# Layer one of a two-layer decoder: the gate computed as [channel, token] and applied after the outputs' transposition, the state updates issued directly behind their products

## The chip, the cores and the metric

The kernel runs on one core of one Trainium2 chip. The metric is the device time of one execution in microseconds (us); the number before is the median of three runs.

Five engines work side by side: PE (TensorE, the matrix engine; PEld is its weight load), DVE (VectorE), ACT (ScalarE), POOL (GpSimd) and SP (SyncE, which here issues all the DMAs). Each works through its own queue in order and waits for others by semaphores.

## The reference, cut to what matters

One sequence of 1024 tokens, model width 1024, mixer width 2048 in 16 heads of 128. Layer one (HGRN2) projects the normalised input into q, forget logits f, values i (v below) and a gate g, runs a gated recurrence over chunks of 64 tokens, normalises each head's output over its 128 channels, and multiplies it by silu(g) before the output projection:

```
q, fz, i, g = jnp.split(h @ w_in, 4, axis=-1)
...
o = _rms(o, onorm_g.reshape(A_HEADS, HEAD_DIM)).reshape(bsz, s, WIDTH).astype(h.dtype)
return (o * jax.nn.silu(g)) @ w_out
```

Layer two (FoX) is a forgetting attention over shared keys and values. The change touches layer one alone.

## The kernel before, in words

All products use float32r operands split into an exact high and low half, so each product of two matrices is three matmuls (high by high, high by low, low by high). `hT(th, k, lo)` is the transposed normalised input, in halves of 512 tokens (`th`) and k-tiles of 128.

There are two forms of a projection. `gemm_T` keeps 128 columns of the weight stationary and moves 512 tokens, so its result is [128 channels, 512 tokens]; one call is 24 matmuls of 128x512. `gemm_N` keeps 128 tokens stationary and moves 256 weight columns, so its result is [128 tokens, 256 channels]; one call covers two token tiles and is 48 matmuls of 128x256. Four calls of either do one projection of a pair of heads over all 1024 tokens.

Layer one goes over eight pairs of heads (`hg_pair`, p = 0 to 7). The main stream of a pair is v (`gemm_N`), g (`gemm_N`), then for each half of the tokens f and q of the pair's two heads (`gemm_T`). `put_g` makes silu(g): a sigmoid on ACT (L577) and a product on DVE (L578). For pair 0, v and half of g grow with the pieces of `hT` while the modulation columns are still being made (`grow`, `lay`).

Beside it run threads. `hg_half(p, th)` does for one half of the tokens: `hg_att` (scores within pairs of chunks and the keys turned round), `hg_state` (the products of keys and values, in PSUM bank `pu`), `hg_out` (the outputs, in bank `po`, normalised by `rsqrt_mean`), and `hg_turn` (the outputs transposed to [channel, token] and stored to `ogd`). The half th = 0 of a pair runs beside the pair's own f and q of th = 1, the half th = 1 beside the next pair's v and g.

The class `Weave` sets PE's order: the main stream calls `tick` with the us that it has laid down, and a thread's next step is put in as soon as its due time is past. PE's order is strict. The order on DVE, ACT, POOL and SP is set when the program is built, by a scheduler that places each instruction by when it estimates that it can run; `tc.high_priority()` raises some.

Names and lines for the steps below. In `hg_forget`: Ln on ACT (L457), the running sum on DVE (L458, a scan), small copies into `dl` (L464 to L466), differences (L467, L468) which the exponentials on ACT (L472) wait for. In `hg_out`: the first state (L520, a copy out of `pu`) and the later ones (L522), each read by the next output matmul; the sums of squares (L525, L527), `rsqrt_mean` (L213 to L219), the scaling (L529, DVE) and the gate's product (L531, POOL, two pieces of 128x256 for each head). In `hg_turn`: the transposes (on PE, recorded at L51), their copy out (L539, ACT) and four stores (L541, SP). `mod_sum` (L260, L263, DVE) works on modulation weights of later layers that stream in beside. `split_w` makes a weight's halves: high on ACT (L224), low on POOL (L225), 128x1024 in each of two pieces; the raw tile is then free for the next load (L236, SP).

Of the kernel before, what the change touches and what calls it, by code (L numbers as in the profile page):

```python
# [8 lines left out]
F32 = mybir.dt.float32  # L9
# [21 lines left out]
class Weave:  # L31
    """The order of the tensor engine: the products of one stream, with the steps of others put in
    between them once enough of the stream has gone by to cover what they wait for."""
# [28 lines left out]
    def tick(self, us):  # L62
        """us of the main stream have been laid down"""
        self.now += us
        while True:
            due = [th for th in self.threads if th[0] <= self.now]
            if not due:
                return
            self._step(min(due, key=lambda th: th[0]))

    def need(self, mark):
        """run the steps on until this mark has been set"""
        while mark not in self.marks:
            assert self.threads, mark
            self._step(self.threads[0])
# [7 lines left out]
def hybrid_trunk_kernel(ctx: ExitStack, tc: tile.TileContext, x, c, mod_w, mod_b, norm_g, a_w_in,  # L83
# [82 lines left out]
    keep = cst.tile([P, P], I32, name="keep")        # 1 where column >= partition  # L166
    V.memset(keep, 1)
    G.affine_select(keep, keep, [[1, P]], ALU.is_ge, 0, base=0, channel_multiplier=-1)
    rows4k = cst.tile([P, D], F32, name="rows4k")    # chunk-reset mask, gate rows, rows of -F
# [38 lines left out]
    def rsqrt_mean(ss, n, inv):  # L208
        """1/sqrt(ss*inv + EPS) on [P, n]: a guess from the exponent, three Newton steps"""
# [12 lines left out]
    def halves(eng, hi, lo, src):  # L222
        """src as a sum of two float32r parts, exactly"""
# [3 lines left out]
    # raw tiles of streamed weights: a list of sources in the order of their use, two loads ahead  # L227
# [12 lines left out]
    def raw_next():  # L240
        """the block of the next raw tile"""
# [7 lines left out]
    def mod_src(b):  # L249
        """modulation weights of output blocks b, b+1 of 128: layer 0, layer 1, kv"""  # L250
# [6 lines left out]
    def mod_sum(*todo):  # L257
        """acc = sum over k-tiles of silu(c) * w, still over partitions, for each (raw tile, acc)"""
# [6 lines left out]
    def mod_cols(b, acc, ps):  # L265
        """mcol[:, b:b+2] = silu(c) @ w + bias"""
# [5 lines left out]
    # h^T as exact float32r halves: block th*4 + k//2, [hi | lo], each [P, 2, 512]  # L272
# [3 lines left out]
    def gscale(gc, sc, k0, k1, g):  # L276
        """g[:, k0:k1] = norm gain * (1 + scale)"""
# [4 lines left out]
    def split_w(eng=None, more=True):  # L282
        """the next raw weight, 256 columns, as exact halves -> accessors of their k-tiles"""
# [9 lines left out]

    def gemm_T(ps, w, j, th):
        """ps[128 outputs, 512 tokens] from columns j*128.. of w"""
        js = slice(j * P, (j + 1) * P)
        for k in range(KT):
            wh, wl = w[0](k)[:, js], w[1](k)[:, js]
            PE.matmul(ps, lhsT=wh, rhs=hT(th, k, 0), start=(k == 0), stop=False)
            PE.matmul(ps, lhsT=wh, rhs=hT(th, k, 1), start=False, stop=False)  # L300
            PE.matmul(ps, lhsT=wl, rhs=hT(th, k, 0), start=False, stop=(k == KT - 1))
            PE.tick(0.65)
# [8 lines left out]
    def gemm_N(ps, w, t):  # L311
        """ps[128 tokens, all columns of w] of token tiles t and t+1"""
# [41 lines left out]
    def h_piece(k, th):  # L354
        """h^T of k-tile k for half of the tokens"""
# [6 lines left out]

    # first weights: v of pair 0 for all tokens and g for half of them grow with the k-tiles of h^T;
    # two token tiles grow side by side in a bank, so a product with zeros opens all of it
# [6 lines left out]
    for ps in vps + gps:  # L371
        PE.matmul(ps, lhsT=zeros[:, 0:P], rhs=zeros, start=True, stop=False)

    def grow(banks, w, i, ts):
        return [(banks, w, k, t) for k in (2 * i, 2 * i + 1) for t in ts]

    def lay(products, pieces):
        """pieces of h^T, with products between them"""
        n = -(-len(products) // len(pieces)) if pieces else len(products)
        while products or pieces:  # L380
            if pieces:
                h_piece(*pieces.pop(0))
            for banks, w, k, t in products[:n]:
                gemm_Nk(c256(banks[t // 2])[:, t % 2, :], w, t, k, False)
# [5 lines left out]
    for i in range(4):  # L390
# [10 lines left out]
        if i == 0:  # L401
            wv = split_w(G, more=False)
            lay([], [(k, 0) for k in ks])
            lay(grow(vps, wv, 0, range(4)), [])
            lay([], [(k, 1) for k in ks])
            ready = grow(vps, wv, 0, range(4, NT))
            continue
        if i == 1:
            wg = split_w(G, more=False)
            ready += grow(gps, wg, 0, range(4))  # L410
        lay(ready, [(k, th) for k in ks for th in range(2)])
        ready = grow(vps, wv, i, range(NT)) + grow(gps, wg, i, range(4))
    lay(ready, [])

    # the other small vectors
# [4 lines left out]
    # lower bound of the first layer: first row of a softmax over the two rows of logits  # L420
# [13 lines left out]
    # units of 512 columns in blocks 18..24  # L434
# [755 lines left out]
```

## Time and profile before

| | us |
|---|---|
| median of three runs (2415.35, 2417.05, 2423.49) | 2417.05 |
| span of the profiled execution | 2421.3 |
| PE busy in it | 2321.1 (96%) |
| DVE busy | 1367.2 (56%) |
| ACT busy | 1004.3 (41%) |
| POOL busy | 594.3 (25%) |

The profile is of one execution. Its span, from the first to the last instruction, is 4.25 us over the median and inside the range of the three runs; what lies around the span is not recorded apart. Layer one's pairs run from about 110 to 1020 us of the span, and a pair takes about 118 us. L48 and L51 are the lines of a helper through which every matmul and every transpose goes, so on PE the tile tells which product it is: `mm` are projections, `oa` outputs, `sm` scores, states and transposes.

### The profile page before, as it was taken

The numbers are of one execution on the slowest core, as the hardware profiler recorded it, in microseconds if no ns is written. First come the engines' busy times: TensorE is split into PE (matmuls) and PEld (weight loads), VectorE is DVE, ScalarE is ACT, GpSimd is POOL, SyncE is SP. The second block draws the span as 40 slices with busy tenths as digits, with TensorE's granted clock in tenths as the row PEclk, the third lists the DMA queues.
The fourth block names the chain that finished last, engine by engine and source line by source line (L and its number), as shares of the span: only waits on it lengthen the run. The fifth ranks groups of instructions, "written<-read, shape, count | busy, mean of one in ns | idle before, by whom it ended". The sixth has DMA issues, their size and how long they took to land.

```text
span 2421.3 us, 39983 instructions
## 1 busy us (share of the span) xinstructions
PE 2321.1 (96%) x15530; PEld 2109.8 (87%) x15530; DVE 1367.2 (56%) x3587; ACT 1004.3 (41%) x1646; POOL 594.3 (25%) x543
## 2 busy tenths in 40 slices
PE   4999999999999999999999999999999999999999
PEld 3889888888888888788899999989999999998887
DVE  7565655555655555746752113267667766777533
ACT  5453444444344435333422222334554544455321
POOL 3222222222222121101321212243343433333000
PEclk9999999999999999999999999999999999999999
DMA  8213131313131313565523322332222322235443
GB/s 276 90 43 98 44 96 45 96 44 97 45 96 53 95 53 108 168 212 173 173 75 111 92 70 83 118 90 85 73 85 63 96 74 85 63 95 176 154 139 116
DMA packets 219970, 245.04 MB, mean 101 GB/s; under 512 B 14547, under 2 KB 182645, under 8 KB 219781
## 3 DMA queue, kind: packets, MB, share of 16 engines
q1 hardware_dynamic: 219780, 242.49, 32.3%
q8 instruction: 122, 2.00, 0.3%
q14 instruction: 68, 0.55, 0.1%
HBM read 196.22 MB, written 46.21 MB: 100 GB/s over the span
## 4 chain that ended last, share of the span: by engine, by line
PE 74%; DVE 12%; ACT 5%; DMA 3%; issue 3%; POOL 2%; SPq 0%; DVEq 0%; ACTq 0%; POOLq 0%
PE mm L48 57%; PE sm L48 6%; PE oa L48 6%; PE sm L51 5%; POOL blk L225 1%; DVE dl L464 1%; DVE rs_y L219 1%; DMA blk<-in_mod_w_dram 1%; DVE blk L225 1%; DVE blk L263 1%; ACT L457 1%; DVE blk L458 1%; DVE rows4k L263 1%; DVE rs_t L214 1%; DVE rs_t L218 1%
## 5 line engine op out<-in xcount | busy, mean ns | idle before, releaser
L48 PE MATMUL mm<-blk,blk 128*128 128x256 f32 (+1 forms) x11408 | 1932.1, 325 | 9.7 <-DVE blk L225 5.3
L48 PEld LDWEIGHTS mm<-blk,blk 128*128 128x128 f32 x11408 | 1650.0, 192 | 158.1 <-DVE blk L225 8.5
L225 POOL TENSOR_TENSOR blk<-blk,blk 128x1024 fp32r<-128x1024 f32 (+1 forms) x134 | 313.9, 2353 | 678.3 <-ACT blk L224 524.3
L224 ACT ACTIVATE blk<-blk 128x1024 fp32r<-128x1024 f32 (+3 forms) x352 | 305.3, 881 | 406.1 <-PE mm L48 264.2
L225 DVE TENSOR_TENSOR blk<-blk,blk 128x1024 fp32r<-128x1024 f32 (+3 forms) x218 | 206.4, 954 | 194.0 <-ACT blk L224 183.1
L51 PE MATMUL sm<-ident,blk 128*128 128x128 f32 x1201 | 188.1, 276 | 36.2 <-POOL blk L531 11.8
L48 PE MATMUL oa<-blk,blk 128*128 128x256 f32 (+1 forms) x1248 | 187.5, 286 | 26.3 <-DVE blk L520 14.6
L48 PE MATMUL sm<-blk,blk 128*128 128x128 f32 (+5 forms) x1456 | 208.6, 301 | 1.3 <-ACT blk L492 1.2
L48 PEld LDWEIGHTS oa<-blk,blk 128*128 128x128 f32 x1248 | 169.9, 193 | 38.2 <-DVE blk L520 15.9
L51 PEld LDWEIGHTS sm<-ident,blk 128*128 128x128 f32 x1201 | 142.0, 141 | 64.5 <-issue 20.6
L48 PEld LDWEIGHTS sm<-blk,blk 128*128 128x128 f32 (+1 forms) x1456 | 168.1, 172 | 19.6 <-issue 3.5
L1034 ACT ACTIVATE blk<-blk,m 128x128 f32<-128x128 f32 (+7 forms) x128 | 99.0, 774 | 127.2 <-DVE m L1032 119.2
L879 DVE TENSOR_REDUCE sst<-blk 128x4 f32<-128x512 f32 x32 | 21.8, 682 | 215.4 <-ACT blk L878 215.4
L1036 POOL TENSOR_SCALAR blk<-blk,smx 128x128 f32<-128x128 f32 (+7 forms) x128 | 98.1, 766 | 136.4 <-DVE smx L1035 123.3
L225 DVE TENSOR_TENSOR blk<-sm,blk 128x512 fp32r<-128x512 f32 (+1 forms) x160 | 92.9, 581 | 62.3 <-ACT blk L224 61.9
L263 DVE SCALAR_TENSOR_TENSOR blk<-blk,cc,blk 128x256 f32<-128x256 f32 x196 | 106.9, 548 | 26.0 <-DMA blk<-in_mod_w_dram 17.2
L1006 POOL TENSOR_TENSOR blk<-rows4k,keep 128x128 f32<-128x128 f32 x128 | 61.5, 480 | 238.0 <-DVE mx L1013 207.7
L224 ACT ACTIVATE blk<-sm 128x512 fp32r<-128x512 f32 (+1 forms) x160 | 81.1, 507 | 48.5 <-PE sm L51 47.8
L1013 DVE CUSTOM_DVE_ANT_0 blk<-sm,rows4k 128x128 f32<-128x128 f32 (+3 forms) x176 | 84.6, 494 | 22.9 <-PE sm L48 21.3
L459 POOL TENSOR_SCALAR blk<-blk,cc 128x512 f32<-128x512 f32 x32 | 23.8, 744 | 251.7 <-ACT blk L456 251.7
L531 POOL TENSOR_TENSOR blk<-blk,blk 128x256 f32<-128x256 f32 x64 | 47.6, 764 | 151.1 <-DVE blk L529 131.4
L472 ACT ACT_TABLE_LOAD x31 | 39.8, 1283 | 102.7 <-DVE blk L467 102.7
(156 smaller groups left out, 1657.4 us busy)
## 6 DMA issues: line engine op xcount, KB each, us to landing
blk<-in_a_w_in_dram SPq DMA_DIRECT2D x64, 512.0 KB, 3.8
blk<-in_mod_w_dram SPq DMA_DIRECT2D x48, 512.0 KB, 4.8
blk<-in_kv_w_dram SPq DMA_DIRECT2D x32, 512.0 KB, 4.5
blk<-in_b_w_in_dram SPq DMA_DIRECT2D x32, 512.0 KB, 3.9
ogd<-blk SPq DMA_DIRECT2D x128, 64.0 KB, 2.2
blk<-in_kv_mod_w_dram SPq DMA_DIRECT2D x16, 512.0 KB, 3.4
blk<-in_a_w_out_dram SPq DMA_DIRECT2D x16, 512.0 KB, 4.9
blk<-ogd SPq DMA_DIRECT2D x16, 512.0 KB, 4.7
```

The lines of the kernel that those rows point to most:

```text
L48: self._chain(self.PE.matmul(*a, **k))
L51: self._chain(self.PE.transpose(*a, **k))
L214: V.tensor_scalar(t.bitcast(I32), m.bitcast(I32), 1, None, ALU.logical_shift_right)
L224: S.activation(hi, src, AF.Copy)
L225: eng.tensor_tensor(lo, src, hi.bitcast(F32), ALU.subtract)
L263: V.scalar_tensor_tensor(acc, rawk(rb, k), csil[:, k:k + 1], acc, ALU.mult, ALU.add)
L472: S.activation(lf[:, :, 1, :], lf[:, :, 1, :], AF.Exp)
L531: G.tensor_tensor(c128(sq)[:, 2 * q:2 * q + 2, :], c128(sq)[:, 2 * q:2 * q + 2, :], sg(th * 4 + 2 * q)[:, :, js], ALU.mult)
L1006: G.tensor_tensor(nfm, nF[:, i * P:n], negm, ALU.add)
L1013: V.tensor_tensor_reduce(dst, src, add, 1.0, -3e38, ALU.add, ALU.max, mx[:, nm:nm + 1])
L1034: S.activation(l[:, 0:n], l[:, 0:n], AF.Exp, bias=m, accum_out=sm)
L1036: G.tensor_scalar(l[:, 0:n], l[:, 0:n], sm, 0.0, ALU.mult, ALU.add)
```

## The change

`gemm_T`'s inner step becomes a function `gemm_Tk`. The gate g is computed by `gemm_T` instead of `gemm_N`, for pair 0's grown half too, and lies as [channel, token] in its block. Its product leaves `hg_out` and is done in `hg_turn`, on the transposed outputs (L545, POOL, one piece of 128x512 for each head), in front of the stores. The state updates move from `hg_out` to `hg_state`, behind the products and under `high_priority`, and `hg_half` first runs the steps on until the previous half's last outputs are laid down. Comments are dropped (not shown).

```
+    def gemm_Tk(ps, w, j, th, k):
+        js = slice(j * P, (j + 1) * P)
+        wh, wl = w[0](k)[:, js], w[1](k)[:, js]
+        PE.matmul(ps, lhsT=wh, rhs=hT(th, k, 0), start=(k == 0), stop=False)
+        PE.matmul(ps, lhsT=wh, rhs=hT(th, k, 1), start=False, stop=False)
+        PE.matmul(ps, lhsT=wl, rhs=hT(th, k, 0), start=False, stop=(k == KT - 1))
...
-    for ps in vps + gps:
+    for ps in vps:
...
+    def grow_g(i):
+        return [(lambda k=k, j=j: gemm_Tk(gps[j], wg, j, 0, k)) for k in (2 * i, 2 * i + 1) for j in range(2)]
...
     def hg_state(j, th, v):
...
-        u["pu"] = pu
-
-    def hg_out(h, j, th, v, sg):
+        with tc.high_priority():
+            if th == 1:
+                V.tensor_scalar(st[:, 0, :], st[:, 0, :], dl[:, 0:1], None, ALU.mult)
+            for n in range(nl):
+                if th == 0 and n == 0:
+                    V.tensor_copy(st[:, 1, :], pu[:, 0:P])
+                else:
+                    V.scalar_tensor_tensor(st[:, (n + 1) % 4, :], st[:, n, :], dl[:, 4 + n:5 + n],
+                                           pu[:, n * P:(n + 1) * P], ALU.mult, ALU.add)
+
+    def hg_out(h, j, th, v):
...
-        for q in range(2):
-            G.tensor_tensor(c128(sq)[:, 2 * q:2 * q + 2, :], c128(sq)[:, 2 * q:2 * q + 2, :],
-                            sg(th * 4 + 2 * q)[:, :, js], ALU.mult)
-
-    def hg_turn(h, j, th):
+
+    def hg_turn(h, j, th, sg):
...
         S.activation(u["ogT"], pg, AF.Copy, scale=ongc[:, h:h + 1])
+        G.tensor_tensor(u["ogT"], u["ogT"], sg(j, th), ALU.mult)
...
+        if p > 0 or th == 1:
+            PE.need(("out", p - 1 + th, 1, 1 - th))
         for j in range(2):
             hg_state(j, th, v)
...
-        for t in range(4 if p == 0 else 0, NT, 2):
-            ps = mm_ps()
-            gemm_N(ps, wg, t)
-            put_g(ps, t)
+        for th in range(1 if p == 0 else 0, 2):
+            for j in range(2):
+                ps = mm_ps()
+                gemm_T(ps, wg, j, th)
+                put_g(ps, j, th)
```

On PE, this is where the gate's products begin beside the half (p = 3, th = 1), just ahead of its second head's outputs. Before (the moving operand stands first behind the arrow: weight blocks 89 to 92, stationary tokens in 71 to 74):

```order
L48 MATMUL mm<-blk_0_89,blk_0_71 128x256
L48 MATMUL mm<-blk_0_91,blk_0_71 128x256
L48 MATMUL mm<-blk_0_89,blk_1_72 128x256
L48 MATMUL mm<-blk_1_90,blk_0_73 128x256
L48 MATMUL mm<-blk_1_92,blk_0_73 128x256
L48 MATMUL mm<-blk_1_90,blk_1_74 128x256
```

Of the change (tokens 69 to 72 move, the weight 89 and 91 is stationary):

```order
L48 MATMUL mm<-blk_0_69,blk_0_89 128x512
L48 MATMUL mm<-blk_1_70,blk_0_89 128x512
L48 MATMUL mm<-blk_0_69,blk_0_91 128x512
L48 MATMUL mm<-blk_0_71,blk_0_89 128x512
L48 MATMUL mm<-blk_1_72,blk_0_89 128x512
L48 MATMUL mm<-blk_0_71,blk_0_91 128x512
```

Half as many matmuls, each twice as wide, stand in the gate's place; where the other products stand between them stays as it was but for a few products' shift.

On DVE, this is the end of the second head's forget work of pair 3, th = 1, where the states of the half (3, 0) are updated (blk_0_115 and blk_1_116 hold the states of the two heads, sm is `pu`). Before:

```order
L458 SCALAR_TENSOR_TENSOR blk_0_107<-rows4k,blk_0_105 128x512
L520 COPY blk_0_115<-sm 128x128
L464 COPY dl<-blk_0_107 128x4
L465 COPY dl<-blk_0_107 128x1
L466 TENSOR_TENSOR dl<-blk_0_107 128x3
L522 SCALAR_TENSOR_TENSOR blk_0_115<-blk_0_115,dl,sm 128x128
L467 TENSOR_TENSOR blk_0_105<-dl,blk_0_107 128x4x64
L468 TENSOR_TENSOR blk_0_107<-blk_0_107,dl 128x4x64
L522 SCALAR_TENSOR_TENSOR blk_0_115<-blk_0_115,dl,sm 128x128
```

Of the change (L465 is the scan, L515 and L517 the states, L471 to L475 the work on `dl` and the differences):

```order
L465 SCALAR_TENSOR_TENSOR blk_0_107<-rows4k,blk_0_105 128x512
L515 COPY blk_0_115<-sm 128x128
L471 COPY dl<-blk_0_107 128x4
L472 COPY dl<-blk_0_107 128x1
L517 SCALAR_TENSOR_TENSOR blk_0_115<-blk_0_115,dl,sm 128x128
L515 COPY blk_1_116<-sm 128x128
L517 SCALAR_TENSOR_TENSOR blk_0_115<-blk_0_115,dl,sm 128x128
L473 TENSOR_TENSOR dl<-blk_0_107 128x3
L517 SCALAR_TENSOR_TENSOR blk_0_115<-blk_0_115,dl,sm 128x128
L474 TENSOR_TENSOR blk_0_105<-dl,blk_0_107 128x4x64
```

The first update stands behind the scan in both; the later ones have moved up past L466 and ahead of the difference (now L474).

On POOL, these are the gate's products of pair 3 among the low halves of weights. Before (L531 is the gate, L225 the low half of a weight piece):

```order
L531 TENSOR_TENSOR blk_1_112<-blk_1_112,blk_0_103 128x256 x2
L225 TENSOR_TENSOR blk_1_92<-blk_1_96,blk_1_90 128x1024
L531 TENSOR_TENSOR blk_1_112<-blk_1_112,blk_0_103 128x256 x2
L225 TENSOR_TENSOR blk_0_87<-blk_0_93,blk_0_85 128x1024
L531 TENSOR_TENSOR blk_1_112<-blk_1_112,blk_1_104 128x256 x2
L225 TENSOR_TENSOR blk_1_88<-blk_1_94,blk_1_86 128x1024
L531 TENSOR_TENSOR blk_1_112<-blk_1_112,blk_1_104 128x256 x2
```

Of the change (L545 is the gate):

```order
L225 TENSOR_TENSOR blk_1_92<-blk_1_96,blk_1_90 128x1024
L545 TENSOR_TENSOR blk_0_117<-blk_0_117,blk_0_103 128x512
L545 TENSOR_TENSOR blk_0_117<-blk_0_117,blk_1_104 128x512
L225 TENSOR_TENSOR blk_0_87<-blk_0_93,blk_0_85 128x1024
L225 TENSOR_TENSOR blk_1_88<-blk_1_94,blk_1_86 128x1024
L545 TENSOR_TENSOR blk_0_117<-blk_0_117,blk_0_103 128x512
L545 TENSOR_TENSOR blk_0_117<-blk_0_117,blk_1_104 128x512
```

The second low half of each weight now stands directly behind the first, ahead of the gate's products. One more exchange, on DVE: `put_g`'s first product of the next pair (before L578, now L585) stood behind the scaling L529 of the second head's th = 1 outputs and now stands ahead of it (now L536).

## Rows read from the trace of the kernel before

**Rows 1.** The page: busy us (share of the span) and instructions.
```profile
PE 2321.1 (96%) x15530; PEld 2109.8 (87%) x15530; DVE 1367.2 (56%) x3587; ACT 1004.3 (41%) x1646; POOL 594.3 (25%) x543
```
**Rows 2.** Groups by form: busy us, mean ns, idle before, what ended it.
```profile
L51 PE MATMUL sm<-ident,blk 128*128 128x128 f32 x1201 | 188.1, 276 | 36.2 <-POOL blk L531 11.8 <-DMA blk<-in_x_dram 9.8 <-DVE blk L883 6.1
...
L48 PE MATMUL oa<-blk,blk 128*128 128x128 f32 x480 | 68.1, 290 | 25.8 <-DVE blk L520 14.6 <-DVE blk L522 11.2
```
**Rows 3.** Timeline of PE, a pair: start, us, instruction, [idle before <-releaser].
```profile
501.39 0.71 PE L48 MATMUL oa<-blk,blk 128*128 128x128 f32 x4 [2.08 <-DVE blk L520]
503.64 1.73 PE L48 MATMUL oa<-blk,blk 128*128 128x128 f32 x6 [1.54 <-DVE blk L522]
...
555.17 3.84 PE L48 MATMUL mm<-blk,blk 128*128 128x256 f32 x30
560.74 0.44 PE L51 MATMUL sm<-ident,blk 128*128 128x128 f32 x2 [1.74 <-POOL blk L531]
561.47 0.46 PE L51 MATMUL sm<-ident,blk 128*128 128x128 f32 x2 [0.30 <-POOL blk L531]
```
**Rows 4.** Chain that ended last, stretches of 256 and of 512 columns: start, us.
```profile
520.64 4.31 PE mm L48 x36
...
594.72 5.49 PE mm L48 x24
```
**Rows 5.** Timeline of DVE: around the wait at 501 us, and later.
```profile
499.79 1.22 DVE L458 TENSOR_TENSOR_SCAN blk<-rows4k,blk 128x512 f32<-128x512 f32 x1 [3.26 <-ACT blk L457]
501.05 0.29 DVE L520 COPY blk<-sm 128x128 f32<-128x128 f32 x1
501.25 1.95 DVE L464 COPY dl<-blk 128x4 f32<-128x4 f32 x1
...
503.18 0.15 DVE L466 TENSOR_TENSOR dl<-blk 128x3 f32<-128x3 f32 x1
...
559.73 0.68 DVE L578 TENSOR_TENSOR blk<-mm,blk 128x512 f32<-128x512 f32 x1
...
584.42 0.17 DVE L464 COPY dl<-blk 128x4 f32<-128x4 f32 x1
```
**Rows 6.** The chain between 546 and 561 us.
```profile
548.65 2.38 POOL blk L225
551.04 4.59 DMA blk<-in_mod_w_dram
...
555.72 0.49 DVE blk L263
...
559.12 0.70 DVE blk L529
...
560.64 0.79 POOL blk L531
```
**Rows 7.** Timeline of POOL.
```profile
500.84 2.34 POOL L225 TENSOR_TENSOR blk<-blk,blk 128x1024 fp32r<-128x1024 f32 x1 [2.42 <-ACT blk L224]
...
543.26 2.40 POOL L225 TENSOR_TENSOR blk<-blk,blk 128x1024 fp32r<-128x1024 f32 x1 [20.02 <-issue]
```
**Rows 8.** Clock windows of PE: stretch, us, PE busy (x), PEclk, DMA share, GB/s.
```profile
210.20:213.60 3.40, 3.40 (x18) 0.50 0.48 128
797.30:800.70 3.40, 3.40 (x19) 0.50 0.37 104
565.20:568.60 3.40, 3.40 (x30) 1.00 0.96 281
...
619.80:626.60 6.80, 5.66 (x18) 0.50 0.25 80
```
**Rows 9.** DVE and POOL at the end of the pairs.
```profile
986.79 2.32 POOL L531 TENSOR_TENSOR blk<-blk,blk 128x256 f32<-128x256 f32 x2 [19.75 <-DVE rs_y L215]
...
987.74 0.70 DVE L217 SCALAR_TENSOR_TENSOR rs_t<-rs_y 128x4 f32<-128x4 f32 x1
```
**Rows 10.** SP's queue: DMA issues.
```profile
563.23 2.06 SPq L541 DMA_DIRECT2D ogd<-blk  x4
565.38 0.43 SPq L236 DMA_DIRECT2D blk<-in_a_w_in_dram  x1
```

More of the change, by code (lines that the diff above doesn't have):

```diff
@@ L292, in split_w @@
         return (lambda k: ar(8 + 2 * i, k * 256, 256, F32R)), (lambda k: ar(9 + 2 * i, k * 256, 256, F32R))
+    def gemm_Tk(ps, w, j, th, k):
[4 more added lines that the diff above has]
+        PE.matmul(ps, lhsT=wl, rhs=hT(th, k, 0), start=False, stop=(k == KT - 1))
     def gemm_T(ps, w, j, th):
-        js = slice(j * P, (j + 1) * P)
         for k in range(KT):
[L298 to L301, printed above, removed]
+            gemm_Tk(ps, w, j, th, k)
             PE.tick(0.65)
@@ L370, in hybrid_trunk_kernel, with grow_v @@
     gps = [sm_ps(), sm_ps()]
-    for ps in vps + gps:
+    for ps in vps:
         PE.matmul(ps, lhsT=zeros[:, 0:P], rhs=zeros, start=True, stop=False)
-    def grow(banks, w, i, ts):
-        return [(banks, w, k, t) for k in (2 * i, 2 * i + 1) for t in ts]
+    def grow_v(i, ts):
+        return [(lambda k=k, t=t: gemm_Nk(c256(vps[t // 2])[:, t % 2, :], wv, t, k, False))
+                for k in (2 * i, 2 * i + 1) for t in ts]
+    def grow_g(i):
+        return [(lambda k=k, j=j: gemm_Tk(gps[j], wg, j, 0, k)) for k in (2 * i, 2 * i + 1) for j in range(2)]
     def lay(products, pieces):
@@ L382, in lay @@
                 h_piece(*pieces.pop(0))
-            for banks, w, k, t in products[:n]:
-                gemm_Nk(c256(banks[t // 2])[:, t % 2, :], w, t, k, False)
+            for product in products[:n]:
+                product()
             del products[:n]
@@ L403, in hybrid_trunk_kernel @@
             lay([], [(k, 0) for k in ks])
-            lay(grow(vps, wv, 0, range(4)), [])
+            lay(grow_v(0, range(4)), [])
             lay([], [(k, 1) for k in ks])
-            ready = grow(vps, wv, 0, range(4, NT))
+            ready = grow_v(0, range(4, NT))
             continue
@@ L409, in hybrid_trunk_kernel @@
             wg = split_w(G, more=False)
-            ready += grow(gps, wg, 0, range(4))
+            ready += grow_g(0)
         lay(ready, [(k, th) for k in ks for th in range(2)])
-        ready = grow(vps, wv, i, range(NT)) + grow(gps, wg, i, range(4))
+        ready = grow_v(i, range(NT)) + grow_g(i)
     lay(ready, [])
@@ L507, in hg_out @@
         pov = c128(po)
-        att, qd, st, dl, pu = u["att"], c128(u["qd"]), c128(u["S"]), u["dl"], u["pu"]
+        att, qd, st = u["att"], c128(u["qd"]), c128(u["S"])
         js = slice(j * P, (j + 1) * P)
-        if th == 1:
-            V.tensor_scalar(st[:, 0, :], st[:, 0, :], dl[:, 0:1], None, ALU.mult)
         for n in range(4):
@@ L516, in hg_out @@
                 PE.matmul(pov[:, n, :], lhsT=qd[:, n, :], rhs=st[:, n, :], start=False, stop=True)
-            if n == 3 and th == 1:
-                break
-            if first:
-                V.tensor_copy(st[:, 1, :], pu[:, 0:P])
-            else:
-                V.scalar_tensor_tensor(st[:, (n + 1) % 4, :], st[:, n, :], dl[:, 4 + n:5 + n],
-                                       pu[:, n * P:(n + 1) * P], ALU.mult, ALU.add)
         sq = u["sq"]
@@ L553, in hg_half @@
         for j in range(2):
-            hg_out(2 * p + j, j, th, v, sg)
+            hg_out(2 * p + j, j, th, v)
             PE.marks.add(("out", p, j, th))
@@ L558, in hg_half @@
         for j in range(2):
-            hg_turn(2 * p + j, j, th)
+            hg_turn(2 * p + j, j, th, sg)
             yield 3.0
@@ L567, in v, with sg, put_g @@
             return ar(bv, t * 256, 256)
-        def sg(t):
-            return c256(ar(bg, t * 256, 512))
+        def sg(j, th):
+            return ar(bg, j * 1024 + th * 512, 512)
         def put_v(ps, t):
             S.activation(ar(bv, t * 256, 512), ps, AF.Copy)
-        def put_g(ps, t):
-            s = ar(bg, t * 256, 512)
-            S.activation(s, ps, AF.Sigmoid)
-            V.tensor_tensor(s, ps, s, ALU.mult)
+        def put_g(ps, j, th):
+            S.activation(sg(j, th), ps, AF.Sigmoid)
+            V.tensor_tensor(sg(j, th), ps, sg(j, th), ALU.mult)
         if p == 0:
@@ L582, in hg_pair @@
                 put_v(vps[t // 2], t)
-            for t in range(0, 4, 2):
-                put_g(gps[t // 2], t)
+            for j in range(2):
+                put_g(gps[j], j, 0)
         else:
@@ L590, in hg_pair @@
         wf = split_w()
-        for t in range(4 if p == 0 else 0, NT, 2):
-            ps = mm_ps()
-            gemm_N(ps, wg, t)
-            put_g(ps, t)
+        for th in range(1 if p == 0 else 0, 2):
+            for j in range(2):
+                ps = mm_ps()
+                gemm_T(ps, wg, j, th)
+                put_g(ps, j, th)
         wq = split_w()
```

## The prediction

> **What bounds the kernel now.** I read the page first: PE is busy for 2321.1 of 2421.3 us [rows 1], so time comes off in three ways only: PE's products take less of it, PE waits less, or its clock is higher. Then the groups of PE by form, for what it waits for in layer one [rows 2]. Two groups matter. The output products (`oa`) wait 25.8 us, for the first states of L520 and the later ones of L522. The transposes (`sm` from `ident`) wait 11.8 us for POOL's gate product of L531; the rest of that group's waits are elsewhere. The timeline of one pair shows where these lie [rows 3]: 2.08 and 1.54 us in front of output products at 501 us, and 1.74 and 0.30 us in front of the second head's transposes at 560 us. Third the clock [rows 8]: 565.2 to 568.6 us holds 30 matmuls of 256 columns at a granted clock of 1.00, the same 3.4 us behind a transposes' wait 18 or 19 at 0.50. [...]
>
> **(a) The gate's products.** A pair's g was 4 calls of 48 matmuls of 128x256, and is 4 calls of 24 of 128x512: 96 a pair, 768 in all. The columns streamed are the same; what can change is the price per instruction. The chain has 36 matmuls of 256 in 4.31 us, 119.7 ns each, and 24 of 512 in 5.49 us, 228.8 ns each [rows 4]. A 512 replaces two 256s and saves 2 x 119.7 - 228.8 = 10.6 ns; x 768 = **8.1 us**. Bounds: a stretch's end is modelled, and taking the 36 as 120 ns or a little less moves the saving by some 20%; pair 0's grown half (48 of the 768) partly stands beside waits, where nothing is won. I keep 6 to 10 us.
>
> [...]
>
> **(b) The transposes' wait.** The second head's transposes are wanted at 559.01 (555.17 + 3.84) and start at 560.74 [rows 3]. They wait for the last link of this chain [rows 6]: the second low half of a weight on POOL (548.65, 2.38 us), which frees the raw block for a load of modulation weights (551.04, 4.59 us), which `mod_sum` on DVE needs at 555.72; behind that in DVE's queue come the Newton steps and the scaling L529 (559.12, 0.70), then L531 (560.64, 0.79). The second pieces of L531 give the 0.30.
>
> After the change the transposes read the scaling's output directly: the 0.79 us of L531 and the 0.30 drop out of PE's path. And on POOL the second low half stands right behind the first, no longer behind the first head's gate. The first runs from 543.26 for 2.40 us [rows 7], so the second can run from 545.66 instead of 548.65: 2.99 us earlier, and with it the load, `mod_sum` and the scaling. Against this, `put_g`'s product, 0.68 us [rows 5], now stands ahead of the scaling. The scaling then ends near 559.82 - 2.99 + 0.68 = 557.5. PE wants it at 559.0 less what (a) has saved in this pair, at most 96 x 10.6 ns = 1.0 us: 558.0. That leaves 0.5 us to spare. What may eat it: while POOL multiplies, small DVE operations can be held up: during L531 at 986.79, L217 took 0.70 us [rows 9], against 0.15 for L466, as small, elsewhere [rows 5]. The first head's new product L545 (I estimate 1.5 us, two pieces of 0.79) runs just among the second head's Newton steps. So a little of the wait can remain: of 11.8 us in seven pairs I leave 0.25 each, and take **10.0 us**. Bounds: 11.8 if nothing holds DVE up, 0 if all of it comes back (rival C).
>
> [...]
>
> **(c) The clock behind those waits.** Three of the seven pairs' waits are followed by 3.4 us at 0.50; the first and the last of the three are shown [rows 8]. Such a stretch does 18 or 19 matmuls instead of 30, so it loses some 11.3 x 0.12 = 1.36 us; three give **4.1 us**. I take it whole, as the wait goes nearly whole; lower bound 0, if the remainder of the wait is enough to lower the clock.
>
> **(d) The state updates.** At 501 us DVE's scan L458 starts at 499.79, having waited 3.26 us for ACT's logarithm, and the state copy L520 stands behind it at 501.05 [rows 5]; PE's output product starts at 501.39 [rows 3]. In the new order the copy (L515) still stands directly behind the scan (now L465), as the excerpt shows: the 2.08 us stay. The second wait, 1.54 us, is for L522, which stood behind L464, and L464 took 1.95 us because POOL's low half ran from 500.84 for 2.34 us [rows 5, 7]. In the new order that small copy (now L471) still stands between the first and the second update; only L466 (0.15 us) has moved behind it. Its start-to-start share can be at most 0.15, at least 0; I take half, in seven pairs (14.6 / 2.08, [rows 2, 3]): **0.5 us**. The clock's falls behind these waits stay as well.
>
> **Costs that I take as nothing.** Three updates now stand ahead of the difference L474, which the exponentials on ACT need; they cost at most three copies' 0.29 us [rows 5], 0.9 us. The first products that read those exponentials come behind pair p + 1's v, and 520 us is still all `mm` [rows 4]: some 14 us of cover. Without it each pair would pay 0.9 us, 7 us in all. The four stores to `ogd` now wait for POOL's L545 (before, for ACT's copy), and they stand in SP's queue ahead of a weight load: 563.23 for 2.06 us, then the load at 565.38 [rows 10]. L545 puts both back by about 1.5 us. That load's weights are split for products from 594 us on, which is their cover; the price if it is gone is rival D. DVE work moved behind others otherwise lies in its idle time (DVE is busy 56%, [rows 1]).
>
> **Sum.** 8.1 + 10.0 + 4.1 + 0.5 = 22.7 us. The profiled execution's 2421.3 would become 2398.6; it lies 4.25 us over the median, and I carry the difference to the median: 2417.05 - 22.7 = **2394 us**.
>
> **Rivals.**
> B, the output waits go too: if the updates, raised in priority, truly ran ahead of the scan, the 25.8 us [rows 2] would go, and the clock's falls behind them, of which one is shown, 619.8 to 626.6, 18 matmuls in 6.8 us [rows 8]. I count seven such stretches, 4 of 3.4 and 3 of 6.8 us, 34 us with 29.4 busy, of which 38% (11.3 of 30) is lost: 11.2 us. 2394 - 25.8 - 11.2 = **2357 us**. For it: the change raises just these instructions. Against it: the order of DVE's queue, which is fixed. Chance 0.09.
> C, the transposes' wait stays: `put_g`'s product ahead of the scaling, and DVE held up by L545, give back what POOL's order won; the clock falls as before. Left are (a) and (d), 8.6 us: **2408 us**. For it: only 0.5 us of spare time. Against it: L531's 0.79 leaves the path whatever DVE does. Chance 0.14.
> [...] Chance 0.05. [...]
> D, slower: the stores that wait for L545 hold SP's in-order queue, the weight load behind them comes late, and PE waits at the head of each pair's f or q. It decides once the lateness exceeds the cover; with a wait as long as the output products' 2.08 + 1.54 in each of 8 pairs, 29 us, it is 2394 + 29 = **2423 us**. Against it: 1.5 us of lateness stands against some 29 us from the load to its products (565 to 594). Chance 0.04.
> Nothing comes of it: equal prices and a wait that moves elsewhere: **2417 us**. Chance 0.04.
>
> **How the numbers follow.** The forecast case has 0.64, its own range 2387 to 2401 ((a) 6 to 10, (b) 7 to 11.8, (c) 0 to 4.1, not all at one end). About 0.3%, 7.25 us, is what a measurement of this kernel can tell from no change: faster is below 2409.8, slower above 2424.3. Faster: 0.64 + 0.09 + 0.05 and most of C (0.11) = 0.89; same: nothing comes of it, the rest of C = 0.07; slower: 0.04, D at its edge and beyond. The range of 8 in 10 goes up over C to 2409 and down to 2380, short of B.
>
> **What would show it.** (a) right: chain stretches of 512 in g at about 229 ns, and PE's busy sum lower by 8 us plus what the clock gives. (b) right: no transposes waiting for POOL, none or a few tenths of a us for DVE's scaling L536; the second low half near 545.7. Wrong: 1 us or more in front of the second head's transposes. (c) right: a granted clock of 0.50 only behind output waits. (d) right: some 2.1 us for L515 and 1.5 for L517 in seven pairs. Without these waits, B was right. SP or a DMA as what ends PE's waits in f or q would be D. Most of all I would be wrong if DVE's queue ran differently than its order and the old durations suggest.

## The result, and the profile after

The changed kernel takes 2385.65 us (median of four runs, 2381.51 to 2386.79); before, on the same chip, 2418.79 us. The ratio is 0.9856, with a 95% interval of 0.984 to 0.9872: 33 us less, where 22.7 us were forecast. That is inside the stated range of 2380 to 2409 us and just below the 2387 to 2401 us that the forecast case had for itself. The profiled execution spans 2384.6 us, 36.7 us less than the one of before.

Where the 36.7 us lie shows on one instruction of DVE, the scan of a pair's second head, seven pairs apart. Before (first two lines) and after:

```profile
147.74 1.23 DVE L458 TENSOR_TENSOR_SCAN blk<-rows4k,blk 128x512 f32<-128x512 f32 x1 [3.26 <-ACT blk L457]
968.10 1.23 DVE L458 TENSOR_TENSOR_SCAN blk<-rows4k,blk 128x512 f32<-128x512 f32 x1 [1.62 <-ACT blk L457]
...
148.56 1.23 DVE L465 TENSOR_TENSOR_SCAN blk<-rows4k,blk 128x512 f32<-128x512 f32 x1 [3.23 <-ACT blk L464]
936.88 1.23 DVE L465 TENSOR_TENSOR_SCAN blk<-rows4k,blk 128x512 f32<-128x512 f32 x1 [1.62 <-ACT blk L464]
```

The seven pairs between took 820.4 us and take 788.3 us: 32.0 us less. The rest lies before and behind them.

The page of the changed kernel, its busy times (us, share of the span, instructions):

```profile
PE 2300.3 (96%) x14760; PEld 2063.2 (87%) x14760; DVE 1373.1 (58%) x3587; ACT 1004.1 (42%) x1646; POOL 587.4 (25%) x511
```

Against [rows 1], PE is busy 20.8 us less, and so 15.9 us of its idle time have gone too. Its groups by form (busy, mean ns, idle before and what ended it):

```profile
L51 PE MATMUL sm<-ident,blk 128*128 128x128 f32 x1201 | 185.9, 275 | 23.7 <-DMA blk<-in_x_dram 9.8 <-DVE blk L891 6.1 <-DVE blk L961 5.0
...
L48 PE MATMUL oa<-blk,blk 128*128 128x128 f32 x480 | 67.4, 291 | 24.6 <-DVE blk L515 14.7 <-DVE blk L517 9.9
```

Of the two waits in [rows 2], the transposes' 11.8 us for POOL are gone altogether, and the output products' 25.8 us are 24.6. The timeline of PE in the same pair, at the places of [rows 3]:

```profile
489.65 0.71 PE L48 MATMUL oa<-blk,blk 128*128 128x128 f32 x4 [2.09 <-DVE blk L515]
491.83 1.65 PE L48 MATMUL oa<-blk,blk 128*128 128x128 f32 x6 [1.47 <-DVE blk L517]
...
542.72 0.60 PE L51 MATMUL sm<-ident,blk 128*128 128x128 f32 x4
543.08 3.70 PE L48 MATMUL mm<-blk,blk 128*128 128x512 f32 x15
546.61 0.60 PE L51 MATMUL sm<-ident,blk 128*128 128x128 f32 x4
```

The second head's transposes at 546.61 wait for nothing. What they read is ready in time, as the timelines of POOL and DVE show:

```profile
531.32 4.71 POOL L225 TENSOR_TENSOR blk<-blk,blk 128x1024 fp32r<-128x1024 f32 x2 [10.51 <-ACT blk L224]
544.17 1.44 POOL L545 TENSOR_TENSOR blk<-blk,blk 128x512 f32<-128x512 f32 x1 [8.14 <-ACT blk L544]
...
531.35 2.38 DVE L219 SCALAR_TENSOR_TENSOR rs_y<-rs_t,rs_y 128x4 f32<-128x4 f32 x1
533.76 2.29 DVE L217 SCALAR_TENSOR_TENSOR rs_t<-rs_y 128x4 f32<-128x4 f32 x1
...
537.22 0.35 DVE L260 TENSOR_SCALAR blk<-blk,cc 128x256 f32<-128x256 f32 x1
...
542.92 0.68 DVE L585 TENSOR_TENSOR blk<-mm,blk 128x512 f32<-128x512 f32 x1
543.52 0.68 DVE L536 TENSOR_TENSOR blk<-oa,rs_y 128x512 f32<-128x512 f32 x1
```

The two low halves of a weight now run one directly behind the other. The second head's scaling L536 ends at 544.20, 2.4 us before PE wants it, and the gate's product L545 starts only as it ends. `mod_sum` begins at 537.22 (L260) without waiting for its load. The low halves now hold up two small steps of the first head's normalisation instead (L219 and L217, 2.38 and 2.29 us, against about 0.16 us elsewhere); that head's transposes come only at 542.72, so PE doesn't wait for it. The chain that ended last has a long stretch of wide products:

```profile
208.47 25.20 PE mm L48 x111
```

That is 227.0 ns each. Last the clock of PE (stretch, us, PE busy, granted clock, DMA share, GB/s); a fall of the clock is a stretch at 0.50:

```profile
266.40:269.80 3.40, 3.40 (x12) 0.51 0.51 154
379.10:382.50 3.40, 3.40 (x12) 0.50 0.48 154
829.60:833.00 3.40, 2.78 (x10) 0.51 0.48 150
150.40:157.20 6.80, 5.66 (x18) 0.50 0.26 77
...
990.10:993.50 3.40, 3.37 (x9) 0.50 0.81 262
```

In layer one the falls to 0.50 are eight now and last 30.7 us in all; before, they were eleven and lasted 51.2 us. The three behind transposes are gone, as forecast, 10.2 us. Those behind output waits are shorter too: of seven, three lasted 6.8 us before [rows 8] and one does now, 27.3 us in all instead of 34.1. And the last one, at the way into the output projection (990.10 above), lasted 6.8 us before:

```profile
1022.60:1029.40 6.80, 5.42 (x15) 0.50 0.72 243
```

These last two differences were not forecast.

### The profile page after: what moved, and what is told of

Same layout as the page of the kernel before. It is cut to its first block, busy times and chain, and to the rows that moved or that the text cites. A ratio compares the mean times of both kernels' runs of the same rounds, so it can differ in the third digit from the quotient of the medians.

```text
span 2384.6 us, 38476 instructions
## 1 busy us (share of the span) xinstructions
PE 2300.3 (96%) x14760; PEld 2063.2 (87%) x14760; DVE 1373.1 (58%) x3587; ACT 1004.1 (42%) x1646; POOL 587.4 (25%) x511
## 4 chain that ended last, share of the span: by engine, by line
PE 82%; DVE 9%; ACT 4%; DMA 2%; issue 2%; POOL 1%; SPq 0%; DVEq 0%; ACTq 0%; POOLq 0%
PE mm L48 65%; PE oa L48 6%; PE sm L48 6%; PE sm L51 5%; DVE dl L471 1%; DVE blk L225 1%; DMA blk<-in_b_w_out_dram 1%; ACT L464 1%; DVE blk L465 1%; DVE rs_t L214 1%; ACT blk L224 1%; DVE blk L263 1%; ACT blk L464 0%; DVE blk L853 0%; POOL blk L225 0%
## 5 line engine op out<-in xcount | busy, mean ns | idle before, releaser
L48 PEld LDWEIGHTS mm<-blk,blk 128*128 128x128 f32 x10688 | 1604.0, 191 | 182.0 <-ACT blk L224 6.7
L225 POOL TENSOR_TENSOR blk<-blk,blk 128x1024 fp32r<-128x1024 f32 (+1 forms) x134 | 312.6, 2343 | 569.5 <-ACT blk L224 567.0
L225 DVE TENSOR_TENSOR blk<-blk,blk 128x1024 fp32r<-128x1024 f32 (+3 forms) x218 | 204.2, 944 | 191.6 <-ACT blk L224 180.0
L48 PEld LDWEIGHTS oa<-blk,blk 128*128 128x128 f32 x1248 | 170.5, 194 | 36.7 <-DVE blk L515 16.0
L225 DVE TENSOR_TENSOR blk<-sm,blk 128x512 fp32r<-128x512 f32 (+1 forms) x160 | 93.0, 581 | 62.2 <-ACT blk L224 61.6
L263 DVE SCALAR_TENSOR_TENSOR blk<-blk,cc,blk 128x256 f32<-128x256 f32 x196 | 111.9, 573 | 20.2 <-DMA blk<-in_mod_w_dram 13.2
L545 POOL TENSOR_TENSOR blk<-blk,blk 128x512 f32<-128x512 f32 x32 | 43.0, 1344 | 237.8 <-ACT blk L544 210.4
L466 POOL TENSOR_SCALAR blk<-blk,cc 128x512 f32<-128x512 f32 x32 | 22.8, 712 | 260.0 <-ACT blk L463 253.4
```

Source lines behind the costliest of these rows:

```text
L48: self._chain(self.PE.matmul(*a, **k))
L225: eng.tensor_tensor(lo, src, hi.bitcast(F32), ALU.subtract)
L263: V.scalar_tensor_tensor(acc, rawk(rb, k), csil[:, k:k + 1], acc, ALU.mult, ALU.add)
L545: G.tensor_tensor(u["ogT"], u["ogT"], sg(j, th), ALU.mult)
```

## The experiments

Each ran beside the kernel before on the same chip. Ratios are to that kernel. The eleven runs are from three chips; beside them and beside the change, the medians of the kernel before were 2418.8 to 2421.3 us, so 2 or 3 us between medians taken beside different ones tell nothing.

**1. The state updates back in the outputs' function.**

```
 def hg_state(j, th, v):
...
-        with tc.high_priority():
-            ... (the updates of st)
+        u["pu"] = pu
 def hg_out(h, j, th, v):
...
+            if first:
+                V.tensor_copy(st[:, 1, :], pu[:, 0:P])
+            else:
+                V.scalar_tensor_tensor(st[:, (n + 1) % 4, :], ...)
 def hg_half(p, th, v, sg):
...
-        if p > 0 or th == 1:
-            PE.need(("out", p - 1 + th, 1, 1 - th))
```

> The change without its third part: the state updates are back in the outputs' function. Theory A (the updates' move is worth nothing, since the first update stands behind the scan either way): output waits of 2.1 and 1.5 us in seven pairs, 30 to 35 us of layer one at a granted clock of 0.50, 2386 us within 2. Rival R (the move is what shortened the clock's falls behind the output waits, from 51 us in all to 31 with the transposes' three gone): 38 to 41 us at 0.50 and 2390 to 2392 us.

Measured 2390.7 us, 0.9881 (0.9868 to 0.9893): 5 us slower than the change by the medians, 6 by the ratios, whose intervals overlap at their ends (0.9868 against 0.9872). The output waits are 2.09 and 1.54 us, and layer one has 41.0 us at 0.50: rival R's numbers. The mean granted clocks of the four executions each, 0.986 to 0.988 here and 0.988 to 0.991 for the change, point the same way. One of its falls on PE's timeline, and in clock stretches beside one that stayed short:

```profile
376.81 1.23 PE L48 MATMUL oa<-blk,blk 128*128 128x128 f32 x4 [2.09 <-DVE blk L528]
379.07 1.72 PE L48 MATMUL oa<-blk,blk 128*128 128x128 f32 x6 [1.03 <-DVE blk L530]
...
376.80:383.60 6.80, 5.76 (x18) 0.50 0.26 77
492.80:496.20 3.40, 3.40 (x11) 0.50 0.50 159
```

The fall at 376.80 begins as the waiting product starts, before the second wait. The one at 492.80 begins 2.4 us behind such a start, when both waits are over.

**2. The state updates' move alone**, made to the kernel before (the edit is the reverse of the one above).

> The kernel before with the third part alone: the state updates behind their products, raised in priority. Theory A: the output waits stay (2.1 and about 1.5 us), the transposes' waits stay, 2416 to 2419 us. Rival R: the falls of the clock behind the output waits get shorter, 2410 to 2414 us. Rival B of the prediction (the updates run ahead of the scan) would be 2380 us.

Measured 2419.18 us, 0.9998 (0.9984 to 1.0013): nothing, as theory A had it, with 47.8 us of layer one at 0.50. So the move has no gain of its own. What it gained in the first experiment depends on the rest of the pair. The twelve executions also show how far one kernel's time can go with the clock: they run from 2407.77 us, at a mean granted clock of 0.991, to 2425.13 us at 0.981. The falls counted in one profile are one sample of that.

**3. The gate's products narrow again.**

```
-            for j in range(2):
-                ps = mm_ps()
-                gemm_T(ps, wg, j, th)
-                put_g(ps, j, th)
+        for t in range(4 if p == 0 else 0, NT, 2):
+            ps = mm_ps()
+            gemm_N(ps, wg, t)
+            put_g(ps, t)
```

> The change with g computed by matmuls of 256 columns again; the gate's product in front of the stores takes those blocks as they lie, so token and channel are mixed up there and the output differs, while every other instruction keeps its size. Theory A (a wide matmul saves 12 ns of two narrow ones, from starts 120 and 228 ns apart): 768 x 12 = 9 us over the change, 2393 to 2397 us. [...] If the narrow products also bring longer falls of the clock back: 2397 to 2400 us.

Measured 2399.13 us, 0.9917 (0.9903 to 0.9932): 15 us over the change. It is the case with longer falls of the clock: there are 41.0 us at 0.50 again. Width and clock can't be separated here; the tenth experiment does it.

**4. POOL's old order, by a dead product.**

```
 def hg_out(h, j, th, v, sg):
...
         V.tensor_tensor(c128(sq), pov, spread(r, 4, P), ALU.mult)
+        for q in range(2):
+            G.tensor_tensor(c128(u["ogT"])[:, 2 * q:2 * q + 2, :], c128(sq)[:, 2 * q:2 * q + 2, :],
+                            c128(sg(j, th))[:, 2 * q:2 * q + 2, :], ALU.mult)
```

> The change with the old gate product of L531 added back on POOL as dead work: it reads the scaled outputs and writes to the tile that the copy behind the transposes overwrites, so PE waits for nothing new, but POOL's order is that of before again, the second low half of a weight behind the first head's product. Theory O (POOL's order clears the wait: the modulation load and the scaling come 3 us earlier): the scaling is 3 us late again, the second head's transposes wait 1.5 to 2 us for DVE's scaling in seven pairs, with falls of the clock behind some: 2396 to 2404 us. Rival L (what cleared the wait is that L531 has left PE's path): waits under 0.5 us, 2385 to 2390 us.

Measured 2396.79 us, 0.9905 (0.9892 to 0.9919). The time is as theory O had it, but the waits are smaller: 3.6 us in seven pairs, 0.34 to 0.88 us each, and one of 1.7 us in the last pair for a modulation column (L269). POOL, DVE and PE in the same pair as above:

```profile
532.68 2.40 POOL L225 TENSOR_TENSOR blk<-blk,blk 128x1024 fp32r<-128x1024 f32 x1 [10.41 <-ACT blk L224]
536.65 1.43 POOL L538 TENSOR_TENSOR blk<-blk,blk 128x256 f32<-128x256 f32 x2 [1.57 <-DVE blk L536]
538.04 2.40 POOL L225 TENSOR_TENSOR blk<-blk,blk 128x1024 fp32r<-128x1024 f32 x1
...
538.72 1.88 DVE L260 TENSOR_SCALAR blk<-blk,cc 128x256 f32<-128x256 f32 x1 [2.19 <-DMA blk<-in_mod_w_dram]
...
544.00 0.48 DVE L263 SCALAR_TENSOR_TENSOR blk<-blk,cc,blk 128x256 f32<-128x256 f32 x1 [1.30 <-DMA blk<-in_mod_w_dram]
...
547.82 0.68 DVE L536 TENSOR_TENSOR blk<-oa,rs_y 128x512 f32<-128x512 f32 x1
...
548.64 0.63 PE L51 MATMUL sm<-ident,blk 128*128 128x128 f32 x4 [0.45 <-DVE blk L536]
```

The second low half is 3 us behind the end of the first again, and `mod_sum` waits twice for its loads (2.19 and 1.30 us), which it doesn't in the change. The scaling ends at 548.50; PE was free for its transposes at 548.19. So its end has moved from 2.4 us ahead of what PE wants to 0.3 us behind: 2.7 us, where the prediction had 2.99. POOL's order does carry the scaling, by the loads; the change had more time to spare than the 0.5 us that I had worked out. While the dead product itself runs (536.65 to 538.08), DVE waits for the first of these loads, so its work, apart from its place, isn't what delays the scaling.

**5. The states truly ahead of the scan.** The second head's scan, and what follows it, is laid down behind the updates and tied to the last of them.

```
+    def hg_decay(h, u, last=None):
+        scan = V.tensor_tensor_scan(u["b"], rst, u["lf"], 0.0, ALU.mult, ALU.add)
+        if last is not None:
+            tc.add_manual_dep(scan.ins, last.ins.name, ..., reason="states first")
...
         for j in range(2):
             hg_state(j, th, v)
+        if th == 0:
+            hg_decay(2 * p + 1, us[1], us[1]["last"])
...
                 hg_forget(2 * p + j, us[j], ps)
+                if th == 0 or j == 0:
+                    hg_decay(2 * p + j, us[j])
```

(`hg_decay` takes over the scan and the rest of `hg_forget` behind it; `last` is the last state update.)

> The change with the second head's scan (and what follows it) tied behind the state updates, for th = 1: DVE, which idles there 3.2 us for ACT's logarithm, does the updates in that time. Theory S (the output waits are only that place in DVE's order): the waits of 2.1 and 1.5 us go in seven pairs, 24 us, with some 0.4 us a pair of starting and stopping, and the falls of the clock behind them, 27 us at half speed, some 12 us: 2344 to 2352 us. Rival N (another wait follows at the same place, for the outputs' bank, the scores or the exponentials, which come later): 2360 to 2385 us.

Measured 2347.2 us, 0.9698 (0.9681 to 0.9715): 38 us under the change, and the fastest version of all. DVE's timeline, to be read against [rows 5]:

```profile
466.63 0.29 DVE L521 COPY blk<-sm 128x128 f32<-128x128 f32 x1
466.96 0.73 DVE L523 SCALAR_TENSOR_TENSOR blk<-blk,dl,sm 128x128 f32<-128x128 f32 x2
...
469.80 1.22 DVE L468 TENSOR_TENSOR_SCAN blk<-rows4k,blk 128x512 f32<-128x512 f32 x1 [0.56 <-ACT blk L464]
471.06 2.21 DVE L477 COPY dl<-blk 128x4 f32<-128x4 f32 x1
```

The updates fill DVE's idle time, and the scan still waits 0.56 us for the logarithm, so its new place costs nothing. PE's output products wait for nothing in layer one, and of its falls of the clock one of 3.4 us is left, at the way into the output projection. This was rival B of the prediction as a mechanism; the change aimed at it by priority and didn't reach it.

**6. The split of the next weight later.**

```
-                nwv = split_w() if p + 1 < NP else None
+                nwv = split_w(after=us[1]["exp"]) if p + 1 < NP else None
```

(`after` ties the split's copies on ACT behind the second head's first exponential.)

> The change with the split of the next pair's first weight tied behind the second head's first exponential, so that POOL's low half of a weight no longer runs while DVE makes its small copy L471. Theory Q (the second output wait is that copy, 1.96 us beside POOL, about 0.2 us alone): the wait of 1.47 us falls to 0.3 us or less in seven pairs, the one of 2.09 stays; 9 to 10 us of waits and up to 10 us of clock: 2366 to 2378 us. Rival W (the copy is slow by itself there, or the split coming later is waited for elsewhere): 2383 to 2390 us.

Measured 2354.2 us, 0.9726 (0.9711 to 0.9741): more than theory Q. Not only the second output wait is gone, but the first too. The profile of the change shows why they are one thing. POOL, DVE and ACT at the first head of the pair, 12 us earlier:

```profile
477.10 2.37 POOL L225 TENSOR_TENSOR blk<-blk,blk 128x1024 fp32r<-128x1024 f32 x1 [2.43 <-ACT blk L224]
...
477.31 2.19 DVE L471 COPY dl<-blk 128x4 f32<-128x4 f32 x1
...
480.16 1.28 ACT L479 ACT_TABLE_LOAD   x1 [3.19 <-DVE blk L474]
```

There the first low half of the weight meets the first head's small copy, and what follows on ACT, up to the second head's logarithm, is late by 2 us. The low half that comes next meets the second head's copy. The split's copies on ACT have moved too, but ACT idles for 3.19 us behind the one of the first head, so they aren't what was late. With the split later, the same two copies on DVE:

```profile
460.68 0.17 DVE L475 COPY dl<-blk 128x4 f32<-128x4 f32 x1
...
470.87 0.16 DVE L475 COPY dl<-blk 128x4 f32<-128x4 f32 x1
```

So both output waits, 3.6 us a pair, came from the two small copies beside POOL. In their place PE now waits 0.9 us a pair for a masked copy of scores on DVE (L499), ahead of which DVE was held up by the later low halves: its small steps of 0.3 to 0.4 us took 2.4 us beside them. A pair is 1.4 to 1.9 us longer than in the fifth experiment, 10.7 us in seven, more than the 7 us that lie between the two as a whole.

**7 and 8. Shifting the pairs in time.** 8 and 15 matmuls more, once.

```
+                if (p, th, j) == (1, 0, 0):
+                    for _ in range(8):
+                        PE.matmul(ps, lhsT=wg[0](0)[:, 0:P], rhs=hT(0, 0, 0), start=True, stop=True)
                 gemm_T(ps, wg, j, th)
```

> The change with 8 matmuls of 512 columns more, once, ahead of pair 1's g (their result is overwritten): 1.8 us of work that moves every later wait. Theory F (how long the clock stays low behind a wait depends on where the wait falls in time; the falls start 1.6 to 2.6 us after the wait's first start and last 3.4 us, and in the first experiment those near 0 us lasted 6.8): at least three of the six falls from pair 2 on last 6.8 us, 38 to 48 us of layer one at 0.50, 2391 to 2397 us. Rival D (the length follows from the wait's size alone): falls of 3.4 us as now, 31 us at 0.50, 2387 to 2388.5 us.

> The same with 15 matmuls, 3.4 us, as much as the shortest fall of the clock lasts. Theory F, if the falls start on steps of that length: the waits stand to them as in the change, falls of 3.4 us, about 31 us at 0.50, 2388 to 2390.5 us, so no slower than with 8 matmuls or faster, though it does more. Rival D: 1.6 us over the run with 8.

Measured 2384.25 us (0.9851, 0.9836 to 0.9867) and 2388.51 us (0.9866, 0.9849 to 0.9882): theory F failed. With 8 matmuls one fall lasted 6.8 us where three or more were forecast. With 15, the time and the 30.7 us at 0.50 came out as forecast, but not for its reason: one fall lasted 6.8 us, at another pair than in the change, and the run is 4.3 us slower than the one with 8. Rival D, the size of the wait, fails as well, by those same long falls: the waits are the same in all pairs of a run, but for what the fall itself takes off the second. Also, the first output wait came 3.2 us earlier in these profiles than in that of the change, before the matmuls were added (that one has a fall of 6.8 us at 58.2 us, ahead of layer one, which these two have not), so a shift of 1.8 us was not what I controlled. What the traces do show, put together: how far behind the start of the first waiting output product the fall begins, and how long it lasts, for all pairs with that wait in eight kernels (before, the change, experiments 1 to 4, 7 and 8):

```
fall lasts   falls   begins behind the product's start by
3.4 us       35      1.6 to 3.2 us
6.8 us       17      -0.1 to 1.2 us
6.8 us        2      1.7 us (both in experiment 1, whose second wait is 1.54 us)
```

So the length goes with the place of the fall against the two waits. The change's pairs from the second on are 112.7 to 112.9 us long, and from pair to pair this distance falls slowly, 2.7, 2.4, 2.1, 1.8, 1.7, 1.6 us: all short. Before, with pairs of 116.5 to 118.6 us, it jumps: 2.8, 0.8, 2.8, 2.3, 0.1, 3.1, 0.6 us, and three are long. Why a distance comes out as it does from a pair's length I have not forecast with success.

**9 to 11. The gate's parts without the output waits.** The scan tied behind the updates as in the fifth experiment, on the kernel before with the updates' move (9), with the narrow gate products of the third (10), and with the dead product of the fourth (11).

> The kernel before with the updates moved and the second head's scan tied behind them, as in the fifth experiment, without the gate's parts. It measures the gate's two parts free of the output waits and of the clock behind them, against the fifth experiment's 2347 us. My account (wide products 8 to 9 us, transposes' waits 11.8 us with some 3 us of starting and stopping, falls of the clock behind some of them 4 to 8 us): 27 to 32 us more, 2374 to 2379 us, transposes' waits of 1.3 to 2 us in seven pairs. [...] Rival G (the gate's parts were worth what the change gained as a whole, 33 us, and the output waits' clock nothing): 2380 us and more.

> The fifth experiment with g by matmuls of 256 columns (token and channel mixed up in the gate's product, as in the third, so the output differs): the width alone, with no output wait whose clock could move. Width 10.6 to 12 ns a wide matmul: 8 to 9 us more than 2347, 2355 to 2357 us. [...] If more than 2359 us, the narrow form has another cost than its starts.

> The fifth experiment with the dead gate product on POOL of the fourth, so with POOL's order of before. If POOL's order is worth what the fourth run showed (waits of 0.3 to 0.9 us for DVE's scaling in seven pairs, 3.6 us, with their starts and stops): 4 to 6 us more, 2351 to 2353 us, more if the clock falls behind them. Rival L (the order costs nothing, and the fourth run's loss was the clock behind the output waits): 2347 to 2348.5 us.

Measured 2374.84 us (0.9815, 0.9799 to 0.9831), 2358.83 us (0.9743, 0.9726 to 0.976) and 2352.56 us (0.9726, 0.9709 to 0.9744). The ninth is as my account had it in the sum: the gate's two parts are worth 28 us by themselves. Not in every term: the falls, for which it had 4 to 8 us, are one of 3.4 us in layer one, and the transposes' waits are 1.0 to 1.9 us a pair. Those waits are the old ones; with them, the scans at both ends of that pair:

```profile
538.30 0.44 PE L51 MATMUL sm<-ident,blk 128*128 128x128 f32 x2 [1.09 <-POOL blk L536]
539.03 0.44 PE L51 MATMUL sm<-ident,blk 128*128 128x128 f32 x2 [0.29 <-POOL blk L536]
...
483.81 1.23 DVE L461 TENSOR_TENSOR_SCAN blk<-rows4k,blk 128x512 f32<-128x512 f32 x1 [0.55 <-ACT blk L457]
594.08 1.23 DVE L461 TENSOR_TENSOR_SCAN blk<-rows4k,blk 128x512 f32<-128x512 f32 x1 [0.56 <-ACT blk L457]
```

The tenth is 11.6 us over the fifth as a whole, more than forecast; but its profile begins with falls before layer one that the other has not, and a wait of 2.0 us for a modulation column (L269) at 134 us. The pairs alone tell the width. One scan in each of two pairs, five pairs apart, in the fifth experiment:

```profile
255.28 1.23 DVE L468 TENSOR_TENSOR_SCAN blk<-rows4k,blk 128x512 f32<-128x512 f32 x1 [0.55 <-ACT blk L464]
...
791.58 1.22 DVE L468 TENSOR_TENSOR_SCAN blk<-rows4k,blk 128x512 f32<-128x512 f32 x1 [0.55 <-ACT blk L464]
```

and in the tenth:

```profile
260.06 1.23 DVE L469 TENSOR_TENSOR_SCAN blk<-rows4k,blk 128x512 f32<-128x512 f32 x1 [0.55 <-ACT blk L465]
...
802.16 1.22 DVE L469 TENSOR_TENSOR_SCAN blk<-rows4k,blk 128x512 f32<-128x512 f32 x1 [0.56 <-ACT blk L465]
```

A pair takes 107.26 us with wide and 108.42 us with narrow products, at full clock and without a wait in both: 1.16 us for 96 wide matmuls, 12.1 ns each, 9.3 us for 768 if pair 0's grown half gains as much. The eleventh has waits of 0.35 to 0.93 us for the scaling again, 3.9 us in seven pairs, no fall of the clock behind them, and 5.4 us more than the fifth. A pair is longer than the fifth's by this wait and some 0.2 us, 5.2 us in seven pairs, and the last pair has a wait of 2.0 us for a modulation column (L269) besides, of which the kernel before has 0.3 us there and the change none. So POOL's order is worth 5 to 7 us here.

## Why the prediction was right, and where it was off

The direction and each mechanism up to (c) held; the sum was 10 us short of the median's 33, and two terms and one statement account for it. That the result still lies inside the stated range is in part luck: no term of the forecast case leads below its own 2387 us, and the 2380 at the range's end was margin.

(a) The width: forecast 8.1 us, measured 9.3 us. The short stretch of wide products in [rows 4] gave 228.8 ns; the long one of after gives 227.0. The pairs of the fifth and the tenth experiment give a saving of 12.1 ns a wide matmul, where the forecast had 10.6. The 0.05 in the sum of the chances goes with a much smaller saving, which no run shows; the runs showed these 12.1 ns. Why a wide matmul costs less than two narrow ones, no run here shows.

(b) The transposes' wait, the largest miss: forecast 10.0 of 11.8 us; all of it went, and more. The step "that leaves 0.5 us to spare" was wrong: 2.4 us were left, since L545 came behind the Newton steps and not among them, and with the weight's low half earlier `mod_sum` no longer waited for its load. And the idle time that a row shows is not all that an interruption costs. In the ninth experiment the pair from 483.8 to 594.1 us (from scan to scan) takes 110.27 us, with 1.38 us of transposes' waits, and a pair of the tenth, without them, 108.42: 1.85 us, so 0.47 us more than the rows say; the other pairs of the ninth without a fall give 0.5 to 0.9 us. At the lower price seven pairs have another 3.3 us, and (b) is some 15 us. That POOL's order does the work, as argued, the fourth and the eleventh experiments show.

(c) The clock: forecast 4.1 us for three falls, all gone. The sentence in (d), "The clock's falls behind these waits stay as well", is the step that failed: they stayed in number, not in length. The 20.5 us less at 0.50 in layer one are six stretches of 3.4 us: the three of (c), two behind output waits, and one at the way into the output projection. At the prediction's 1.36 us each that is 8.2 us, of which 2.7 and 1.4 us were in no term.

(d) The output waits stayed, for the reason given; the second lost 0.07 us a pair, as forecast.

With the 1.2 us that the output waits' rows lost and another 1.2 us of a wait for ACT's L492 that is gone, the terms are 9.3 + 15.1 + 8.2 + 1.2 + 1.2 = 35.0 us of the profiled executions' 36.7. What of it falls into the seven pairs, some 31 us (width 7.7, as the tenth against the fifth in the same pairs, 15.1, five stretches 6.8, the output waits' rows 1.0), can be held against the 32.0 us that these pairs lost. The rest is not assigned; the start of layer one differs by 3 us between profiles.

Rival B was ruled out on good grounds, the order of DVE's queue. Its price was right, 37 us for the output waits and the falls behind them: the fifth experiment took 38 us off the change. Rival D had nothing to it: PE never waits there for SP. Of the state updates the prediction said that they gain next to nothing; alone they gain nothing (second experiment), beside the gate's parts 5 to 6 us (first), through the length of the clock's falls. That this length hangs on where a wait falls is shown by the eight traces; that 0.07 us of wait a pair is what moved it in the first experiment is only argued.

## What to carry to other kernels

Raising the priority of an instruction need not change its place: here it stayed behind a scan that waits 3.2 us. Read its place in the engine's queue, and if it stands behind a long wait, tie that one behind it (38 us here). Before moving work off a waiting engine, look for what holds up the tiny instructions at the head of its chain: two copies of four columns, each 2 us late beside POOL, were behind all of the output waits. And price a wait by the length of a whole period with and without it, not by the idle rows alone: the start, the stop and the clock behind it can be as much again (the ninth's pair with a fall: 1.75 us of rows, and 3.7 us longer than the tenth's).

## What the runs showed of the hardware

The same two waits are followed by 3.4 us (35 falls) or by 6.8 us (19 falls) at a granted clock of 0.50, by where the fall begins between them (table above). The state updates' move, which gains nothing alone (2419.18 us, 0.9998), comes with 5 to 6 us beside the gate's parts: 30.7 us of layer one at 0.50 in the change, 41.0 us without the move. One kernel's executions differ by more: the twelve of the second experiment lie between 2407.77 us (mean granted clock 0.991) and 2425.13 us (0.981).

A copy of 128x4 on DVE takes 2.19 us beside POOL's product of 128x1024 (L471 at 477.31 in the change) and 0.17 us without it (L475 at 460.68 in the sixth experiment). The sixth experiment shows how far these 2 us travel: through the exponentials to the next head's logarithm, and to PE, whose output waits of 3.6 us a pair are gone in it.
